# Merging transfers in a hybrid attention layer: spills, doubled loads, broadcast reciprocals, row statistics and mixed values

## The chip, the cores and the metric

The kernel runs on one core of a Trainium2 chip. The metric is the device time of one execution in microseconds (us). Before the change it was 1261.07 us, the median of 3 runs (1257.18 to 1261.21). A difference of about 0.3% is what a measurement of this kernel can tell from none.

## The reference

One decoder layer on 2048 tokens of width 1024, in float32:

```python
hdn  = rmsnorm(x, norm_gain)
proj = hdn @ w_in                 # q, k, v, gate of mixer A and of mixer B
q, k = rope(rmsnorm(q)), rope(rmsnorm(k))            # per head, both mixers
o_a  = banded_attention(q_a, k_a, v_a, 127, sinks)   # 8 heads, 2 kv heads
o_b  = dilated_attention(q_b, k_b, v_b)              # 8 heads
x    = x + concat([o_a * silu(g_a), o_b * silu(g_b)]) @ w_out
```

`banded_attention` lets a query read the keys of a causal band and returns its output, its row maximum and its softmax denominator. `dilated_attention` runs it three times, with (window, dilation) of (128, 1), (512, 4) and (2048, 16), on tokens gathered by stride, and merges the three outputs weighted by their denominators.

## The kernel before, in words

The layer is worked off in eight stages (`STAGES`, L26): four stages "B", each for two heads of mixer B, two stages "A", each for four heads of mixer A, and two stages "O" for the two halves of the output projection. A stage goes over four blocks `sb` of 512 tokens, a block over two halves of 256 tokens. Tokens are kept in a permuted order: within a block of 512, tokens of the same residue mod 4 lie together.

Every product of float32 values is made of three TensorE products (`mm3`, L241): both sides are split into a high and a low part. `proj` (L246) is a generator that makes the projections of a block step by step; while it runs, the attention units of earlier work are worked off between its steps (`advance`, L931), in a proportion set by hand-written costs. A unit has the steps scores, transposes, pv and after, and for a dilated unit a load that is called when the unit is among the next two pending. Actions on the list `late` are counted down in ticks and run some steps later. The compiler's planner then sets the order of the instructions on each engine by its own model of durations.

All transfers are issued by SyncE (`nc.sync.dma_start`) and so stand in one queue in the order of the program: a transfer that has to wait for a semaphore holds up those behind it. The steps that the change touches:

- **Spills** (`finish`, L342). At the end of a B block, q, k, the low parts of k, and the gate are stored to DRAM tensors `qd`, `kd`, `ld`, `gd`, so that the dilated units can read them back by residue r. For q and k there is one store for each of the two heads (L360, L362). V is stored as it is made (`vd`, L315): its source has 128 partitions, its destination is the access pattern [4, 32, 256] (residue, row, element).
- **Row statistics** (`units_B`, L750). The window units of a B block leave row maxima and denominators in `scB`. Four stores (L760), one for each residue, put them in `sd`, laid out [4, 32, 4, 4, 4], in runs of 16 bytes; one load of 32 KB (L859) reads them for the whole stage into `s1c` (128 partitions of 64 values).
- **Dilated loads** (`units_D`, L771, `load` in `dil`). A dilated unit for residue r and head h loads `cq`, `ck`, `cl` and `cv`, each with two buffers. The k of a head has 64 rows; it is needed twice, in partitions 0 to 63 and 64 to 127, and so `ck` (L785) and `cl` (L788) are each loaded by two transfers of 64 partitions x 2 KB. The scores' matmuls at L808 and L809 read them.
- **Broadcast reciprocals.** After its two dilated units, the weights of a residue are transposed to 16 rows, stored to a small DRAM tensor `rD` (L881), and read back with each row repeated over 64 partitions, in the tile `Rb` (one buffer): twice, for the two patterns (`bcast`, L887), each time by two transfers of 64 partitions. GpSimd multiplies with them at L899 and L904. In mixer A, `final` (L678) does the same with `rA`, once for each pair of heads, for the product at L688.
- **Mixed values.** The gated outputs are stored to `mx`, eight DRAM tensors (L93), one for each 256 tokens: four stores for a dilated residue (L909), two for a pair of heads of mixer A (L690). Stages "O" load them as their x (`x_load`, L145).

Of the kernel before, what the change touches and what calls it, by code (L numbers as in the profile page):

```python
# [18 lines left out]
KC = DM // 128  # L19
# [9 lines left out]
def f32(ap):  # L29
    return ap.bitcast(F32)  # L30
# [3 lines left out]
def hybrid_layer(ctx, tc, xT, xn, x, wB, wA, wO, ng, gains, sinks, rot, masks, ident, out):  # L34
# [55 lines left out]
                nc.gpsimd.tensor_scalar(zt, mk[z, 0:640], 0.0, None, op0=OP.mult)  # L90

    rs_row = [dram([256], f"rsr{hf}") for hf in range(8)]
    mx = [dram([128, KC, 256], f"mx{hf}") for hf in range(8)]  # L93

    def bcast_row(d, lo, n, parts=128):
        return bass.AP(tensor=d.tensor, offset=d.offset + lo, ap=[[0, parts], [1, n]])
# [131 lines left out]
    def spill_tiles(si):  # L228
        if si not in spill:
            spill[si] = {  # L230
                "q": dram([2, 4, 128, 512], f"qd{si}"),
                "k": dram([2, 4, 64, 512], f"kd{si}"),
                "l": dram([4, 128, 512], f"ld{si}"),
                "v": dram([4, 4, 128, 256], f"vd{si}"),
                "g": dram([4, 128, 512], f"gd{si}"),
                "o": dram([4, 128, 512], f"od{si}"),
                "s": dram([4, 32, 4, 4, 4], f"sd{si}"),
            }
        return spill[si]

# [101 lines left out]
    def finish(si, sb, half, hls):  # L342
        kind = STAGES[si][0]
        KK, KL = K[si, sb]
        nk = 1 if kind == "A" else 2
        if half == 0 and sb > 0:
            pk, pl = K[si, sb - 1]
            for h in range(nk):
                nc.scalar.activation(KK[:, h, :, 0, :], f32(pk[:, h, :, 4, :]), AF.Copy)
            for h in range(nk):  # L350
                hs = slice(64 * h, 64 * h + 64)
                nc.scalar.activation(KL[hs, h, :, 0, :], f32(pl[hs, h, :, 4, :]), AF.Copy)
        yield from qk_transposes(si, sb, half, hls)
        if half == 0:
            return
        if kind == "B":
            d = spill_tiles(si)
            cs = slice(sb * 128, sb * 128 + 128)
            for h in range(2):
                nc.sync.dma_start(d["q"][h][:, :, cs].rearrange("r p c -> p r c"),  # L360
                                  f32(Q[si, sb][1][:, h]))
                nc.sync.dma_start(d["k"][h][:, :, cs].rearrange("r p c -> p r c"),  # L362
                                  f32(KK[:64, h, :, 1:5, :]).rearrange("p r i u -> p r (i u)"))
            for h in range(2):
                hs = slice(64 * h, 64 * h + 64)
                nc.sync.dma_start(d["l"][:, hs, cs].rearrange("r p c -> p r c"),
                                  f32(KL[hs, h, :, 1:5, :]).rearrange("p r i u -> p r (i u)"))
            nc.sync.dma_start(d["g"][:, :, cs].rearrange("r p c -> p r c"),
                              G[si, sb][0].rearrange("p r i u -> p r (i u)"))
            pending.extend(units_B(si, sb))  # L370
            if sb == 3:
                pending.extend(units_D(si, 0))
        else:
            pending.extend(units_A(si, sb))
# [281 lines left out]
    def units_A(si, sb):  # L656
        idx = STAGES[si][1]
        sc = wk.tile([128, 2, 4, 4], F32, name="scA")
        units = []
        osum = {}  # L660

        def rows(p):
            e = wk.tile([128, 2, 4], F32, name="eA")
            hs = slice(2 * p, 2 * p + 2)
            nc.vector.tensor_tensor(e, sc[:, 0, hs], sk[:, 4 * idx + 2 * p:4 * idx + 2 * p + 2, None].to_broadcast([128, 2, 4]),
                                    op=OP.add)
            nc.scalar.activation(e, e, AF.Exp)
            nc.vector.tensor_tensor(e, e, sc[:, 1, hs], op=OP.add)
            nc.vector.reciprocal(e, e)
            pr = ps.tile([8, 128], F32, name="po", bufs=2)  # L670
            nc.tensor.transpose(pr, e.rearrange("p h i -> p (h i)"), idf)
            rr = wk.tile([16, 128], F32, name="rr")
            nc.scalar.activation(rr[:8], pr, AF.Copy)
            d = dram([8, 128], f"rA{si}_{sb}_{p}")
            nc.sync.dma_start(d, rr[:8])
            osum["d", p] = d

        def final(p):  # L678
            d = osum["d", p]
            rb = wk.tile([128, 512], F32, name="Rb", bufs=1)  # L680
            for a in range(2):
                nc.sync.dma_start(rb[64 * a:64 * a + 64, :],
                                  bass.AP(tensor=d.tensor, offset=d.offset + a * 512, ap=[[0, 64], [1, 512]]))
            t = osum[p]
            g = G[si, sb][p].rearrange("p r i u -> p (r i u)")
            nc.gpsimd.tensor_tensor(t, t, g, op=OP.mult)
            mix = wk.tile([128, 512], F32, name="o1c", bufs=1)
            nc.gpsimd.tensor_tensor(cm_view(mix), cm_view(t), to_cm(rb), op=OP.mult)  # L688
            for a in range(2):
                nc.sync.dma_start(mx[2 * sb + a][:, 2 * idx + p, :], mix[:, 256 * a:256 * a + 256])  # L690

        for p in range(2):
            units.extend(pair_units(si, sb, p, sc, osum, rows, final))
        return units
# [55 lines left out]
    def units_B(si, sb):  # L750
        sc = wk.tile([128, 4, 2, 2], F32, name="scB")
        osum = wk.tile([128, 512], F32, name="osum", bufs=3)
        d = spill_tiles(si)
        units = []
        for h in range(2):
            def after(h=h):
                if h == 1:
                    with nc.allow_non_contiguous_dma(reason="row statistics"):
                        for r in range(4):
                            nc.sync.dma_start(d["s"][:, :, sb, r, :].rearrange("i u k -> u i k"),  # L760
                                              sc[32 * r:32 * r + 32].rearrange("p i a h -> p i (a h)"))
                    cs = slice(sb * 128, sb * 128 + 128)
                    nc.sync.dma_start(d["o"][:, :, cs].rearrange("r p c -> p r c"), osum.rearrange("p (r c) -> p r c", r=4))
            stats = ([sc[:, i, 0, h:h + 1] for i in range(4)], [sc[:, i, 1, h:h + 1] for i in range(4)])
            units.append(window_unit(si, sb, h, stats, cm_view(osum[64 * h:64 * h + 64, :]), after))
        return units


    S1 = {}

    def units_D(si, r):  # L771
        d = spill_tiles(si)
# [3 lines left out]
        def dil(h):  # L776
# [3 lines left out]
            def load():  # L780
                q = wk.tile([128, 512], F32R, name="cq")
                nc.sync.dma_start(f32(q), d["q"][h, r])
                k = wk.tile([128, 512], F32R, name="ck")
                for a in range(2):
                    nc.sync.dma_start(f32(k[64 * a:64 * a + 64, :]), d["k"][h, r])  # L785
                kl = wk.tile([128, 512], F32R, name="cl")
                for a in range(2):
                    nc.sync.dma_start(f32(kl[64 * a:64 * a + 64, :]), d["l"][r, hp:hp + 64, :])  # L788
                v = wk.tile([128, 4, 128], F32R, name="cv")
                nc.sync.dma_start(f32(v), d["v"][r][:, :, 128 * h:128 * h + 128].rearrange("t p e -> p t e"))  # L790
                s["v"], s["q"], s["k"], s["kl"] = v, q, k, kl
# [62 lines left out]
            def after():  # L854
                if h == 0:
                    return
                if (si) not in S1:
                    t = wk.tile([128, 4, 4, 4], F32, name="s1c")
                    nc.sync.dma_start(t.rearrange("p s r k -> p (s r k)"), d["s"].rearrange("i u s r k -> (i u) (s r k)"))  # L859
                    S1[si] = t  # L860
                s1 = S1[si]
                A = s1[:, :, r, :].rearrange("p t (k h) -> p k h t", k=2)
# [23 lines left out]
                o2 = c["o2"]  # L886
                def bcast(k):  # L887
                    rb = wk.tile([128, 512], F32, name="Rb", bufs=1)
                    for a in range(2):
                        nc.sync.dma_start(rb[64 * a:64 * a + 64],  # L890
                                          bass.AP(tensor=dd.tensor, offset=dd.offset + 1024 * k + a * 512, ap=[[0, 64], [1, 512]]))
                    return rb

                def first():
# [8 lines left out]
                def third(rb):  # L903
                    nc.gpsimd.tensor_tensor(o2, o2, rb, op=OP.mult)  # L904
                    nc.gpsimd.tensor_tensor(o2, o2, o1, op=OP.add)
                    nc.gpsimd.tensor_tensor(o2, o2, gc, op=OP.mult)
                    ch = 4 + STAGES[si][1]
                    for t_ in range(4):
                        nc.sync.dma_start(mx[2 * t_ + r // 2][:, ch, 128 * (r % 2):128 * (r % 2) + 128],  # L909
                                          o2[:, 128 * t_:128 * t_ + 128])  # L910

                late.append([2, first])

# [126 lines left out]
```

## Time and profile before

| what | value |
|---|---|
| time, median of 3 runs | 1261.07 us (1257.18 to 1261.21) |
| time of the profiled execution | 1261.51 us |
| its span, first to last instruction | 1259.4 us |
| TensorE matmul busy | 1174.8 us, 93% of the span |
| VectorE, ScalarE, GpSimd busy | 850.7, 834.7, 680.4 us |
| granted TensorE clock | 0.969 |
| DMA queue q1 | 219.37 MB, its packets took 59.3% of the 16 DMA engines' time |
| chain that ended last | PE 55%, DMA 16%, DVE 10%, ACT 8%, POOL 6%, issue 3%, SPq 2% |

PE is TensorE, DVE VectorE, ACT ScalarE, POOL GpSimd, SP or SPq SyncE and its queue. L785 is line 785 of the kernel. In names such as `ck<-kd`, the tile written stands before the arrow and what is read behind it. The chain that ended last is followed back from the last instruction, at each step to what released it; a share of it is time in which that engine, or a transfer's landing, was what the end waited for. A share of DMA is the part of the time for which the 16 DMA engines worked on packets; a packet is one run of bytes that one engine moves.

### The profile page before, as it was taken

Reading aid. Unit: us, or ns where it says so; the run is one execution under the profiler, and the core shown is the slowest. Engines: PE = TensorE matmul, PEld = TensorE weight load, DVE = VectorE, ACT = ScalarE, POOL = GpSimd, SP = SyncE. Lnnn points to the kernel's source line nnn. Section 1 sums busy time; section 2 is a strip of 40 time slices with the busy share of each in tenths; the row PEclk is TensorE's granted clock in tenths of the full one; section 3 lists DMA queues with packets and bytes.
Section 4 is the critical chain, followed back from the end, with each engine's and each line's share of the span. In section 5 each row is a group of like instructions: output and inputs, shape, how many; then the busy total and the mean of one; then the engine's idle time right before and its main releaser. Section 6 shows DMA issues by size and latency. Waiting matters only on the chain.

```text
span 1259.4 us, 25438 instructions
## 1 busy us (share of the span) xinstructions
PE 1174.8 (93%) x8328; PEld 1141.3 (91%) x8328; DVE 850.7 (68%) x2288; ACT 834.7 (66%) x2418; POOL 680.4 (54%) x788
## 2 busy tenths in 40 slices
PE   6898979899899798899998999999999999999899
PEld 5898979899799798888997999898899998999898
DVE  5676768678677678776777788789868877522221
ACT  6477868678677687676777677677776776522221
POOL 4886734566645574536576567565655554333122
PEclk9899989999899899899998999999999999999999
DMA  7454677877687667687775764545333225566561
GB/s 215 120 166 127 193 226 212 229 200 212 182 250 207 210 190 201 189 244 204 199 210 172 228 203 143 150 137 167 114 97 94 80 89 165 163 192 211 166 191 69
DMA packets 196883, 220.98 MB, mean 175 GB/s; under 512 B 34312, under 2 KB 143632, under 8 KB 196752
## 3 DMA queue, kind: packets, MB, share of 16 engines
q1 hardware_dynamic: 196752, 219.37, 59.3%
q8 instruction: 66, 1.08, 0.4%
q14 instruction: 65, 0.53, 0.1%
HBM read 164.44 MB, written 54.86 MB: 174 GB/s over the span
## 4 chain that ended last, share of the span: by engine, by line
PE 55%; DMA 16%; DVE 10%; ACT 8%; POOL 6%; issue 3%; SPq 2%; POOLq 0%; ACTq 0%; DVEq 0%
PE pj L244 39%; DMA xs<-in_xT 3%; DMA Rb<-rD 2%; DMA stg<-in_wB 2%; PE po L849 2%; DMA stg<-in_wO 2%; DMA stg<-in_wA 2%; PE sc L590 1%; PE sc L591 1%; PE po L645 1%; PE pt L828 1%; PE po L735 1%; PE pt L719 1%; ACT P L599 1%; DVE ptl L574 1%
## 5 line engine op out<-in xcount | busy, mean ns | idle before, releaser
L244 PE MATMUL pj<-wh,xh 128*128 128x384 f32 (+1 forms) x1008 | 332.8, 332 | 12.2 <-ACT wh L104 5.5
L244 PE MATMUL pj<-wl,xh 128*128 128x384 f32 (+1 forms) x1008 | 334.4, 332 | 0.8 <-DVE wl L102 0.7
L244 PE MATMUL pj<-wh,xl 128*128 128x384 f32 (+1 forms) x1008 | 333.4, 331 | 1.3 <-DVE xl L157 1.3
L157 POOL TENSOR_TENSOR xl<-xs,xh 128x512 fp32r<-128x512 f32 x158 | 210.3, 1341 | 146.3 <-ACT xh L155 136.6
L155 ACT ACTIVATE xh<-xs 128x512 fp32r<-128x512 f32 x252 | 154.5, 629 | 123.6 <-PE pj L244 100.6
L244 PEld LDWEIGHTS pj<-wh,xh 128*128 128x128 f32 x1008 | 194.0, 193 | 15.7 <-ACT wh L104 5.8
L244 PEld LDWEIGHTS pj<-wl,xh 128*128 128x128 f32 x1008 | 194.8, 193 | 3.2 <-DVE wl L102 1.1
L244 PEld LDWEIGHTS pj<-wh,xl 128*128 128x128 f32 x1008 | 194.4, 193 | 3.0 <-DVE xl L157 1.6
L574 DVE TENSOR_TENSOR ptl<-pt,pth 128x512 fp32r<-128x512 f32 (+3 forms) x232 | 142.0, 619 | 35.5 <-ACT pth L573 31.8
L244 PE MATMUL pj<-xh,wgh 128*128 128x256 f32 x496 | 147.7, 298 | 17.9 <-DVE V L311 12.0
L244 PE MATMUL pj<-xh,wgl 128*128 128x256 f32 x496 | 145.8, 294 | 0.0
L244 PE MATMUL pj<-xl,wgh 128*128 128x256 f32 x496 | 145.4, 293 | 0.0
L573 ACT ACTIVATE pth<-pt 128x512 fp32r<-128x512 f32 (+3 forms) x232 | 123.1, 543 | 23.1 <-PE pt L719 8.1
L431 POOL TENSOR_TENSOR t<-t,t 128x256 f32<-128x256 f32 (+1 forms) x96 | 78.1, 814 | 77.9 <-DVE t L422 57.2
L244 PEld LDWEIGHTS pj<-xh,wgh 128*128 128x128 f32 x496 | 97.8, 197 | 19.7 <-ACT klz L502 5.9
L244 PEld LDWEIGHTS pj<-xl,wgh 128*128 128x128 f32 x496 | 97.8, 197 | 0.6
L244 PEld LDWEIGHTS pj<-xh,wgl 128*128 128x128 f32 x496 | 97.4, 196 | 0.9 <-DVE wgl L105 0.2
L814 ACT ACTIVATE P<-P,scD 128x256 f32<-128x256 f32 (+3 forms) x128 | 71.6, 560 | 33.6 <-DVE scD L813 32.9
L157 DVE TENSOR_TENSOR xl<-xs,xh 128x512 fp32r<-128x512 f32 x94 | 76.9, 823 | 21.1 <-ACT xh L155 20.5
L447 DVE TENSOR_TENSOR t<-t,fac 128x256 f32<-128x256 f32 (+1 forms) x96 | 67.4, 710 | 30.8 <-POOL fac L182 23.7
L182 POOL TENSOR_TENSOR fac<-un,mhalf 128x8 f32<-128x8 f32 (+1 forms) x48 | 85.4, 1779 | 2.5
L813 DVE CUSTOM_DVE_ANT_0 P<-sc,mk 128x256 f32<-128x256 f32 (+3 forms) x128 | 61.1, 484 | 32.2 <-PE sc L809 31.5
(188 smaller groups left out, 3082.8 us busy)
## 6 DMA issues: line engine op xcount, KB each, us to landing
xs<-in_xT SPq DMA_DIRECT2D x94, 512.0 KB
xs<-mx SPq DMA_DIRECT2D x32, 512.0 KB
vd<-V SPq DMA_DIRECT2D x64, 128.0 KB
qd<-qc SPq DMA_DIRECT2D x32, 256.0 KB
TT<-tab SPq DMA_DIRECT2D x32, 256.0 KB
cv<-vd SPq DMA_DIRECT2D x32, 256.0 KB
cq<-qd SPq DMA_DIRECT2D x32, 256.0 KB
ck<-kd SPq DMA_DIRECT2D x64, 128.0 KB
```

The costliest lines, as they stand in the source:

```text
L155: nc.scalar.activation(h, f, AF.Copy)
L157: eng.tensor_tensor(l, f, f32(h), op=OP.subtract)
L182: nc.gpsimd.tensor_tensor(y, u, mhalf.to_broadcast([128, n]), op=OP.pow)
L244: nc.tensor.matmul(o, a, b, start=first and n == 0, stop=last and n == 2, skip_group_check=True)
L431: nc.gpsimd.tensor_tensor(t1[:, :n], t1[:, :n], t2[:, :n], op=OP.add)
L447: nc.vector.tensor_tensor(t1v, t1v, fac[:, tt, :, None].to_broadcast([128, nh, 64]), op=OP.mult)
L573: nc.scalar.activation(hi, pt, AF.Copy)
L574: nc.vector.tensor_tensor(lo, pt, f32(hi), op=OP.subtract)
L590: nc.tensor.matmul(sc[:, j, :], q[h // 2][:, h % 2, i, :], kw, start=True, stop=False)
L813: nc.vector.tensor_tensor_reduce(pd, o[:, :m], m2[:, 512 - m:], -0.125, BIG, OP.add, OP.min, nb)
L814: nc.scalar.activation(pd, pd, AF.Exp, bias=nb, scale=-1.0, accum_out=l)
L849: nc.tensor.matmul(po[:, o:o + w], a, b, start=n_ == 0, stop=n_ == len(seq) - 1, skip_group_check=True)
```

## The change

Transfers that move several parts of one tensor are made one:

- the q and k spills of both heads: one store each, with head and residue as one dimension;
- the two halves of `ck`, and of `cl`: one load of 128 partitions from a source that is read twice by a leading dimension of 2 with step 0 (`twice`);
- the two halves of `Rb`: one load from a source [2, 64 with step 0, 512];
- the row statistics: one store of 128 partitions x 64 bytes for each block, in a layout [4, 128, 16]; the gathering is moved to the load, which becomes four loads of 32 partitions in runs of 16 bytes;
- the mixed values: `mx` becomes one DRAM tensor with a leading dimension of 8, and the four or two stores one.

The diff, with unchanged lines left out:

```diff
-    mx = [dram([128, KC, 256], f"mx{hf}") for hf in range(8)]
+    mx = dram([8, 128, KC, 256], "mx")
...
-                "s": dram([4, 32, 4, 4, 4], f"sd{si}"),
+                "s": dram([4, 128, 16], f"sd{si}"),
...
-            for h in range(2):
-                nc.sync.dma_start(d["q"][h][:, :, cs].rearrange("r p c -> p r c"),
-                                  f32(Q[si, sb][1][:, h]))
-                nc.sync.dma_start(d["k"][h][:, :, cs].rearrange("r p c -> p r c"),
-                                  f32(KK[:64, h, :, 1:5, :]).rearrange("p r i u -> p r (i u)"))
+            nc.sync.dma_start(d["q"][:, :, :, cs].rearrange("h r p c -> p (h r) c"),
+                              f32(Q[si, sb][1]).rearrange("p h r c -> p (h r) c"))
+            nc.sync.dma_start(d["k"][:, :, :, cs].rearrange("h r p c -> p (h r) c"),
+                              f32(KK[:64, :, :, 1:5, :]).rearrange("p h r i u -> p (h r) (i u)"))
...
-            for a in range(2):
-                nc.sync.dma_start(rb[64 * a:64 * a + 64, :],
-                                  bass.AP(tensor=d.tensor, offset=d.offset + a * 512, ap=[[0, 64], [1, 512]]))
+            nc.sync.dma_start(rb, bass.AP(tensor=d.tensor, offset=d.offset, ap=[[512, 2], [0, 64], [1, 512]]))
...
-            for a in range(2):
-                nc.sync.dma_start(mx[2 * sb + a][:, 2 * idx + p, :], mix[:, 256 * a:256 * a + 256])
+            nc.sync.dma_start(mx[2 * sb:2 * sb + 2, :, 2 * idx + p, :].rearrange("a p n -> p a n"),
+                              mix.rearrange("p (a n) -> p a n", a=2))
...
-                        for r in range(4):
-                            nc.sync.dma_start(d["s"][:, :, sb, r, :].rearrange("i u k -> u i k"),
-                                              sc[32 * r:32 * r + 32].rearrange("p i a h -> p i (a h)"))
+                        nc.sync.dma_start(d["s"][sb], sc.rearrange("p i a h -> p (i a h)"))
...
+    def twice(dst, src):
+        nc.sync.dma_start(dst, bass.AP(tensor=src.tensor, offset=src.offset, ap=[[0, 2]] + [list(x) for x in src.ap]))
...
-                for a in range(2):
-                    nc.sync.dma_start(f32(k[64 * a:64 * a + 64, :]), d["k"][h, r])
+                twice(f32(k), d["k"][h, r])
...
-                for a in range(2):
-                    nc.sync.dma_start(f32(kl[64 * a:64 * a + 64, :]), d["l"][r, hp:hp + 64, :])
+                twice(f32(kl), d["l"][r, hp:hp + 64, :])
...
-                    nc.sync.dma_start(t.rearrange("p s r k -> p (s r k)"), d["s"].rearrange("i u s r k -> (i u) (s r k)"))
+                    ds = d["s"]
+                    with nc.allow_non_contiguous_dma(reason="row statistics"):
+                        for i in range(4):
+                            nc.sync.dma_start(t[32 * i:32 * i + 32].rearrange("u s r k -> u (s r) k"),
+                                              bass.AP(tensor=ds.tensor, offset=ds.offset + 4 * i,
+                                                      ap=[[16, 32], [512, 16], [1, 4]]))
...
-                    for a in range(2):
-                        nc.sync.dma_start(rb[64 * a:64 * a + 64],
-                                          bass.AP(tensor=dd.tensor, offset=dd.offset + 1024 * k + a * 512, ap=[[0, 64], [1, 512]]))
+                    nc.sync.dma_start(rb, bass.AP(tensor=dd.tensor, offset=dd.offset + 1024 * k, ap=[[512, 2], [0, 64], [1, 512]]))
...
-                    for t_ in range(4):
-                        nc.sync.dma_start(mx[2 * t_ + r // 2][:, ch, 128 * (r % 2):128 * (r % 2) + 128],
-                                          o2[:, 128 * t_:128 * t_ + 128])
+                    nc.sync.dma_start(mx[r // 2::2, :, ch, 128 * (r % 2):128 * (r % 2) + 128].rearrange("t p n -> p t n"),
+                                      o2.rearrange("p (t n) -> p t n", t=4))
```

## The prediction

> **What bounds the kernel now.** I read the page's totals first, then the table of stretches, then the chain of waits, then the DMA views.
>
> ```profile
> span 1259.4 us, 25438 instructions
> PE 1174.8 (93%) x8328; PEld 1141.3 (91%) x8328; DVE 850.7 (68%) x2288; ACT 834.7 (66%) x2418; POOL 680.4 (54%) x788
> DMA packets 196883, 220.98 MB, mean 175 GB/s; under 512 B 34312, under 2 KB 143632, under 8 KB 196752
> q1 hardware_dynamic: 196752, 219.37, 59.3%
> PE 55%; DMA 16%; DVE 10%; ACT 8%; POOL 6%; issue 3%; SPq 2%; POOLq 0%; ACTq 0%; DVEq 0%
> ```
>
> TensorE is busy for 93% of the span and holds 55% of the chain that ended last; SyncE's own issuing (SPq) holds 2% of it, about 25 us. All transfers go through one hardware queue, q1, whose packets keep the 16 DMA engines busy for 59.3% on average. So PE sets the time, with DMA landings (16% of the chain) as its main interruptions. The profiled execution took 1261.51 us (2.1 us around the span), 0.04% from the median of 1261.07, so sums made against it need no correction.
>
> The table of stretches (start:end, length, busy time of PE, PEld, DVE, ACT, POOL, clock, DMA share, GB/s) shows where DMA has least room:
>
> ```profile
> 172.00:880.00 708.00, 661.74 (x4540) 640.42 (x4539) 532.86 (x1482) 525.32 (x1548) 409.67 (x482) 0.96 0.69 198
> 880.00:1010.00 130.00, 127.16 (x925) 123.06 (x925) 100.70 (x297) 94.42 (x304) 73.46 (x80) 1.00 0.31 98
> ```
>
> From 172 to 880 us the dilated units run (their loads, the broadcast reciprocals); there the engines are 69% busy as a mean, and PE 661.74 of 708 us. There is 31% of slack if transfers stay spread over all 16 engines, and none if many land on a few.
>
> **How a transfer is spread.** This is the point on which the forecast turns, and the trace can be made to tell it. The list of DMA issues has 48 rows that add up to 1136 transfers; these are its first, those with a special shape, and its last:
>
> ```profile
> xs<-in_xT SPq DMA_DIRECT2D x94, 512.0 KB
> ...
> vd<-V SPq DMA_DIRECT2D x64, 128.0 KB
> ...
> TT<-in_rot SPq DMA_DIRECT2D x16, 128.0 KB
> ...
> sd<-scB SPq DMA_DIRECT2D x64, 2.0 KB
> ...
> rA<-rr SPq DMA_DIRECT2D x16, 4.0 KB
> ...
> rsr<-RB SPq DMA_DIRECT2D x8, 1.0 KB
> s1c<-sd SPq DMA_DIRECT2D x4, 32.0 KB
> ...
> ngt<-in_ng SPq DMA_DIRECT2D x1, 4.0 KB
> sk<-in_sinks SPq DMA_DIRECT2D x1, 4.0 KB
> ```
>
> By their shapes, the data runs under 512 B are sd 64 x 128, s1c 4 x 128, TT<-in_rot 16 x 512, and ngt and sk 128 each: 17,152. The page counts 34,312 packets under 512 B, so 17,160 small packets are not data. One completion packet per engine and transfer would make 1136 x 16 = 18,176; 1016 are missing. That is exactly 64 x 12 + 16 x 8 + 8 x 15: the vd stores, whose destination counts 4 in its outermost dimension, run on 4 engines, the rA stores (8 rows) on 8, the rsr stores (1 row) on 1, all others on 16. An access pattern's outermost count limits the engines, although the other side of vd has 128 partitions.
>
> **The change part by part.**
>
> *Doubled dilated loads (`twice`, ck and cl).* Two issues of 128 KB become one of 256 KB whose source is led by a dimension of 2 with step 0. The 128 issues become 64 merged loads. *Broadcast reciprocals (Rb):* the source is now led by [512, 2]; 64 issues from rD become 32, and 32 from rA become 16. By the count just made, each of these 112 merged transfers runs on 2 engines, and each of the two moves 64 rows of 2 KB, 131,072 bytes, where 16 engines moved 8 rows each before. The rate of one engine comes from q1's packets, bytes and share in three windows: 172 to 880, 1200 to 1250 (few small packets, some queueing) and 1180 to 1185 us (almost none):
>
> ```profile
> q1 hardware_dynamic: 137961, 139.41, 68.7%
> q1 hardware_dynamic: 2929, 6.96, 42.0%
> q1 hardware_dynamic: 368, 0.66, 35.5%
> ```
>
> 139.41 MB / (0.687 x 16 x 708 us) = 17.9 KB/us; 6.96 / (0.42 x 16 x 50) = 20.7; 0.66 / (0.355 x 16 x 5) = 23.2. A merged transfer holds its two engines for 7.3, 6.3 or 5.6 us, against about 0.8 us on each of 16 at 20.7.
>
> Now the stretch 172 to 880. It contains all ck, cl and rD transfers and, of rA, these:
>
> ```profile
> ck<-kd SPq DMA_DIRECT2D x64, 128.0 KB
> cl<-ld SPq DMA_DIRECT2D x64, 128.0 KB
> Rb<-rD SPq DMA_DIRECT2D x64, 128.0 KB
> vd<-V SPq DMA_DIRECT2D x47, 128.0 KB
> Rb<-rA SPq DMA_DIRECT2D x8, 128.0 KB
> ```
>
> So 32 + 32 + 32 + 4 = 100 merged transfers, 26.2 MB, that is 13.1 MB on each of two engines. The rest, 139.4 - 26.2 = 113.2 MB, puts 7.08 MB on every engine; the 47 vd stores put 1.16 MB more than an even share on four engines. If the two are always the same, and among vd's four, they carry 13.1 + 7.08 + 1.16 = 21.3 MB: 920 us of work at 23.2, 1031 at 20.7, 1192 at 17.9, in a stretch of 708. It grows by 212, 323 or 484 us. No row names the engine of a packet; I take the same two, since nothing in the rows suggests a rotation, and leave the other to a rival. I take the middle rate: the high one would need no queueing and two engines that never idle, the low one today's contention on all 16, which falls when 14 of them wait. **+323 us.** PE, with 662 us of work there, then waits for the two engines.
>
> [...]
>
> What is late next shows in the chain of waits around 404 us (start, length, what) and in the waits of that stretch:
>
> ```profile
> 404.46 5.18 DMA vd<-V
> ...
> 410.59 3.47 DMA rD<-rr
> ...
> 414.62 3.58 DMA Rb<-rD
> ...
> 418.34 1.30 POOL o1c L899
> ...
> 420.18 4.38 DMA Rb<-rD
> POOL o1c L899 <- DMA Rb<-rD: 58.3, 15, 8.2
> DVE P L813 <- PE sc L809: 31.5, 28, 3.4
> SPq L890 <- DMA rD<-rr: 34.7, 14, 5.3
> ```
>
> SyncE waits for rD to land before it issues Rb, and for POOL's L899 before the second Rb; behind it in its queue stand the next xs, cq and ck loads. Each Rb landing grows by some 5.5 us (6.3 - 0.8) plus the backlog, and every 16-engine transfer behind it lands only when its shares on the two loaded engines do. Those waits are how the stretch is stretched; they are inside the +323, not on top of it.
>
> *After 880* twelve merged rA broadcasts remain at +5.5 us, 66 us if each were on the path, nothing if POOL's idle time hid all. The engines are 31% busy there, and PE 127 of 130 us; a landing that is late by 5.5 us is mostly hidden by POOL's 44% of idle time, so a quarter: **+16 us**. Without that cover it is the 66.
>
> *Spills of q and k, mixed values, row statistics.* q and k spills: 64 issues become 32; mixed values: 64 become 16 and 32 become 16; both are rewritten with the partition outermost on both sides (128, or 64 for k), so 16 engines and the same runs. Row statistics: 64 stores become 16 with runs of 64 B in place of 16 B; 4 loads become 16 of 512 runs of 16 B: 10,240 small runs against 8704, all on 16 engines. In all 244 fewer of the 1136 issues:
>
> ```profile
> L785 SPq DMA_DIRECT2D ck<-kd x64: 444/473/1381, 172.6 to 787.2; - x64
> L890 SPq DMA_DIRECT2D Rb<-rD x64: 444/509/678, 211.7 to 869.8; - x64
> L760 SPq DMA_DIRECT2D sd<-scB x64: 302/426/1807, 86.7 to 703.8; - x64
> ```
>
> At about 0.47 us an issue (medians, ns) that is 115 us of SyncE's time, but SyncE mostly waits for others; of the chain it is 25 us, and 244/1136 of that is **-5 us** (bounds 0 and -25). `mx` as one tensor could make a mixed-value store wait, at the head of SyncE's queue, for an earlier one where its eight parts were tracked apart: such a wait is 2.5 us by the nearest row (34.7 us in 14 for L890), so 80 us for the 32 stores, and 0 if regions are told apart. I take 0, since an earlier store has long landed when the next is made, and keep the 80 as a bound.
>
> Sum: 1261.5 + 323 + 16 - 5 = 1595 us. Its own range: 1261.5 + 212 - 25 = 1450 to 1261.5 + 484 + 66 + 80 = 1890, the last only with all upper ends at once.
>
> **The rivals.**
>
> 1. *Not slower: the write side alone sets the spread.* In all three shapes that the trace shows on few engines, the destination is the short side, or both are; no row has a short source before a 128-partition destination, as here. If the source does not count, all merged transfers stay on 16 engines, 244 issues go, and each Rb pair lands one issue (0.51 us) sooner on some of the 32 rD steps: -5 to -25, about 1246 us. It decides if the number of completion packets stays at 16 for ck, cl and Rb. Against it: a source led by 2 has to be cut somehow, and vd shows that the shorter of the two counts won. 10%.
>
> 2. *Latency only: two engines per transfer, but different ones.* Then no pair of engines overflows, and each merged landing is just 5.5 us later. The whole chain has Rb<-rD 2.5% (31.5 us, some nine landings of 3.58): +50; the 28 waits of L813 behind the scores that read ck and cl: +154 if all grow. Between them about +100: 1360 us. For it: no row names the engines. Against it: a rotation would have to be kept somewhere. 10%.
>
> 3. *Worse: the two engines also idle.* SyncE, in order, stands at L890 while they drain. If they were busy for only 80% of the stretch, 1031 / 0.8 = 1289 us, +581: 1850 us. For it: the SP waits above, and PE and DMA each waiting for the other with two buffers per name. Against it: a backlog of 10 us outlasts most of those waits (5.3 us at the longest). 8%.
>
> ```profile
> by line: PE pj L244 38.9%; issue 3.5%; DMA xs<-in_xT 2.6%; DMA Rb<-rD 2.5%; DMA stg<-in_wB 2.2%; PE po L849 2.1%; DMA stg<-in_wO 1.9%; DMA stg<-in_wA 1.6%; PE sc L590 1.4%; PE sc L591 1.4%; PE po L645 1.3%; PE pt L828 1.3%; PE po L735 1.3%;
> ```
>
> **How the numbers follow.** Forecast 72%, rivals 10, 10 and 8%. The range reaches from 1400 (the forecast's low end, and the upper part of rival 2) to 1800: it leaves out rival 1, most of rivals 2 and 3, and of the forecast only its far upper end. About 0.3% is what a measurement of this kernel can tell from no change. Faster takes most of rival 1 (7%), the same its rest and a rival 2 that is hidden (4%), slower the remaining 89%.
>
> **What would show it.** Right: 892 issues with 892 x 16 - 1016 - 112 x 14 = 11,688 completions and 18,688 small data runs, 30,376 packets under 512 B; the mean DMA share falls while the span grows; Rb, ck and cl landings of 7 us and more head the chain of waits; the growth lies between the first dilated load and the last, and the stretches before 172 us hardly change. Rival 1: 31,944 such packets, and unchanged landings. Rival 2: two completions, but PE's idle time only next to L808, L899 and L904. The forecast is wrong in size if the stretch of the dilated units grows by less than 212 or more than 484 us.

## The result, and the profile after

The changed kernel takes 1625.22 us (median of 4 runs, 1624.22 to 1628.3), against 1261.14 us before (median of 4). The ratio is 1.2888, with a 95% interval of 1.2837 to 1.2938: slower by 364 us. The forecast was 1595 us in a range of 1400 to 1800.

The page of the kernel after, the lines that answer to the first fence of the prediction:

```profile
span 1623.0 us, 25100 instructions
PE 1248.7 (77%) x8328; PEld 1205.8 (74%) x8328; DVE 829.6 (51%) x2288; ACT 837.8 (52%) x2418; POOL 666.9 (41%) x788
DMA packets 192945, 220.94 MB, mean 136 GB/s; under 512 B 30376, under 2 KB 139696, under 8 KB 192816
q1 hardware_dynamic: 192816, 219.35, 45.1%
DMA 34%; PE 30%; issue 9%; POOL 8%; ACT 8%; DVE 7%; SPq 4%; POOLq 0%; ACTq 0%; DVEq 0%
```

Packets under 512 B are 30,376, the number that the prediction gave for two engines per merged transfer (31,944 would have meant 16). The same bytes are moved, the mean busy share of the DMA engines falls from 59.3 to 45.1%, and yet DMA landings are now 34% of the chain that ended last and PE only 30%: the DMA engines as a whole are emptier, and the end waits for a few of them.

The tables of stretches follow, with the columns of the prediction's table (start:end, length, PE, PEld, DVE, ACT, POOL, clock, DMA share, GB/s). The first is of after: first dilated load to last mixed-value store of a dilated residue, then the rest, then what lies before. The second is of before, for the two parts that the prediction did not show:

```profile
168.00:1222.00 1054.00, 725.68 (x4553) 694.43 (x4551) 512.20 (x1483) 528.06 (x1550) 395.24 (x481) 0.83 0.45 133
1222.00:1623.00 401.00, 375.78 (x2840) 366.90 (x2840) 203.03 (x535) 191.03 (x548) 155.27 (x148) 0.96 0.41 129
0.00:168.00 168.00, 147.28 (x937) 144.51 (x938) 114.37 (x272) 118.76 (x321) 116.42 (x159) 0.92 0.59 171
```

```profile
0.00:172.00 172.00, 146.81 (x953) 142.84 (x954) 115.90 (x277) 119.92 (x327) 115.65 (x159) 0.94 0.58 170
880.00:1259.00 379.00, 366.22 (x2839) 358.07 (x2838) 201.95 (x530) 189.47 (x544) 155.06 (x148) 0.99 0.43 136
```

The stretch of the dilated units grew from 708 to 1054 us (+346), the rest from 379 to 401 (+22), and what lies before changed by -4. Counting the packets of q1 in the traces tells what filled the added time: exactly two packets are in flight for 351 of these 1054 us, against 11 of the 708 before. By the small packets a merged transfer has two engines, so nearly all of the added time, 340 of 346 us, is time in which only two DMA engines work.

The chain that ended last in after, where the first dilated loads are made (start, length, what):

```profile
174.91 14.94 DMA cq<-qd
...
201.86 13.12 DMA cl<-ld
...
226.26 9.78 DMA xs<-in_xT
...
239.55 9.78 DMA rD<-rr
```

Some of its longer waits (who waited for what: us in total, times, longest):

```profile
POOL o1c L898 <- DMA Rb<-rD: 217.0, 15, 24.3
...
DVE P L809 <- PE sc L805: 123.8, 33, 19.3
...
SPq L890 <- DMA rD<-rr: 64.7, 16, 8.1
SPq L890 <- DMA Rb<-rD: 59.4, 12, 7.2
```

The shapes of cq, xs and rD were not touched, and by the count of 30,376 small packets they still run on 16 engines. They land after 9.8 to 14.9 us; before, the chain had 3.5 us for rD. That some of their shares stand behind merged transfers is the reading that fits; the view of one line below supports it. SyncE shows a second thing. Its timeline (start, length of the issue, line, count) at the same place:

```profile
168.39 1.19 SPq L767 DMA_DIRECT2D ck<-kd  x1
169.67 0.78 SPq L767 DMA_DIRECT2D cl<-ld  x1
170.50 4.35 SPq L767 DMA_DIRECT2D ck<-kd  x1
174.91 5.44 SPq L780 DMA_DIRECT2D cq<-qd  x2
180.39 1.34 SPq L767 DMA_DIRECT2D cl<-ld  x1
181.78 5.36 SPq L148 DMA_DIRECT2D xs<-in_xT  x1
...
202.52 10.58 SPq L858 DMA_DIRECT2D s1c<-sd  x4
```

An issue takes about 0.45 us in the median, before and after; here single issue instructions last 4.4 and 5.4 us. All issues added took 544 us for 1136 transfers before and 704 us for 892 after.

By 174.9 us, then, three merged transfers have been issued (`ck`, `cl`, `ck`). In the window 173 to 180 us q1 shows this (packets, MB, share of the 16 DMA engines):

```profile
q1 hardware_dynamic: 173, 0.35, 12.8%
```

12.8% of 16 is 2.05 engines. Merged transfers on different pairs would have kept four or six engines busy, 25% or more. So these merged transfers, queued together, ran on the same two engines, one after the other, and the other fourteen had nothing to do in this window. The two moved 0.35 MB in 7 us, 25 KB/us each: at that rate, a merged transfer alone holds them for 5.2 us, an estimate from the 131,072 bytes that each of them moves for it.

### The profile page after: what moved, and what is told of

Its sections match the earlier page's. It is cut to its first block, busy times and chain, and to the rows that moved or that the text cites. A ratio compares the mean times of both kernels' runs of the same rounds, so it can differ in the third digit from the quotient of the medians.

```text
span 1623.0 us, 25100 instructions
## 1 busy us (share of the span) xinstructions
PE 1248.7 (77%) x8328; PEld 1205.8 (74%) x8328; DVE 829.6 (51%) x2288; ACT 837.8 (52%) x2418; POOL 666.9 (41%) x788
## 2 busy tenths in 40 slices
DMA packets 192945, 220.94 MB, mean 136 GB/s; under 512 B 30376, under 2 KB 139696, under 8 KB 192816
## 3 DMA queue, kind: packets, MB, share of 16 engines
q1 hardware_dynamic: 192816, 219.35, 45.1%
## 4 chain that ended last, share of the span: by engine, by line
DMA 34%; PE 30%; issue 9%; POOL 8%; ACT 8%; DVE 7%; SPq 4%; POOLq 0%; ACTq 0%; DVEq 0%
PE pj L244 22%; DMA Rb<-rD 7%; DMA xs<-in_xT 4%; DMA rD<-rr 4%; DMA cl<-ld 4%; DMA Rb<-rA 3%; DMA cq<-qd 3%; DMA stg<-in_wB 2%; DMA stg<-in_wO 2%; ACT P L598 2%; POOL fac L182 2%; SPq L767 1%; DMA cv<-vd 1%; DVE ptl L573 1%; ACT xh L155 1%
## 5 line engine op out<-in xcount | busy, mean ns | idle before, releaser
L244 PE MATMUL pj<-wh,xh 128*128 128x384 f32 (+1 forms) x1008 | 343.8, 343 | 43.1 <-DVE G L332 24.2
L244 PE MATMUL pj<-wh,xl 128*128 128x384 f32 (+1 forms) x1008 | 342.1, 340 | 8.6 <-POOL xl L157 8.3
L244 PE MATMUL pj<-wl,xh 128*128 128x384 f32 (+1 forms) x1008 | 341.6, 339 | 0.8 <-DVE wl L102 0.7
L244 PEld LDWEIGHTS pj<-wh,xh 128*128 128x128 f32 x1008 | 201.6, 201 | 48.0 <-DVE G L332 24.8
L244 PEld LDWEIGHTS pj<-wh,xl 128*128 128x128 f32 x1008 | 201.9, 200 | 10.6 <-POOL xl L157 9.1
L809 DVE CUSTOM_DVE_ANT_0 P<-sc,mk 128x128 f32<-128x128 f32 (+3 forms) x128 | 61.0, 484 | 140.3 <-PE sc L805 123.8
L810 ACT ACTIVATE P<-P,scD 128x128 f32<-128x128 f32 (+3 forms) x128 | 71.5, 559 | 110.0 <-DVE scD L809 109.7
L244 PEld LDWEIGHTS pj<-xh,wgh 128*128 128x128 f32 x496 | 104.8, 211 | 22.9 <-ACT ob L734 9.5
L898 POOL TENSOR_TENSOR o1c<-o1c,Rb 128x512 f32<-128x512 f32 x16 | 20.4, 1272 | 223.6 <-DMA Rb<-rD 217.0
L804 PE MATMUL sc<-ck,cq 128*128 128x256 f32 (+2 forms) x128 | 48.2, 382 | 76.2 <-DMA cq<-qd 45.6
```

Of the source, the lines that this page charges most:

```text
L244: nc.tensor.matmul(o, a, b, start=first and n == 0, stop=last and n == 2, skip_group_check=True)
L804: nc.tensor.matmul(o, q[:, qs], k[:, :n], start=True, stop=False)
L809: nc.vector.tensor_tensor_reduce(pd, o[:, :m], m2[:, 512 - m:], -0.125, BIG, OP.add, OP.min, nb)
L810: nc.scalar.activation(pd, pd, AF.Exp, bias=nb, scale=-1.0, accum_out=l)
```

## The experiments

The differences below are between medians, each against runs of the kernel before that were made together with it. The compiler's planner orders the instructions anew for each version, so a difference can also come from the order. In the traces, TensorE's order differs from that of before at 42% of its places in the first run below and at 52% in the run with k on 128 rows, and these two are within 0.4% of before: a new order alone need not cost anything.

**The rest of the change alone.** The kernel after, with the merged loads undone:

```diff
-                twice(f32(k), d["k"][h, r])
+                for a in range(2):
+                    nc.sync.dma_start(f32(k[64 * a:64 * a + 64, :]), d["k"][h, r])
...
-                twice(f32(kl), d["l"][r, hp:hp + 64, :])
+                for a in range(2):
+                    nc.sync.dma_start(f32(kl[64 * a:64 * a + 64, :]), d["l"][r, hp:hp + 64, :])
...
-            nc.sync.dma_start(rb, bass.AP(tensor=d.tensor, offset=d.offset, ap=[[512, 2], [0, 64], [1, 512]]))
+            for a in range(2):
+                nc.sync.dma_start(rb[64 * a:64 * a + 64, :],
+                                  bass.AP(tensor=d.tensor, offset=d.offset + a * 512, ap=[[0, 64], [1, 512]]))
...
-                    nc.sync.dma_start(rb, bass.AP(tensor=dd.tensor, offset=dd.offset + 1024 * k, ap=[[512, 2], [0, 64], [1, 512]]))
+                    for a in range(2):
+                        nc.sync.dma_start(rb[64 * a:64 * a + 64],
+                                          bass.AP(tensor=dd.tensor, offset=dd.offset + 1024 * k + a * 512, ap=[[0, 64], [1, 512]]))
```

> The kernel after with ck, cl and Rb taken back to two 64-partition transfers each; the merged spills, row statistics and mixed values stay. Theory (two engines carry the merged ck, cl and Rb): the whole loss goes, and 132 fewer issues than before leave 1261 - 5, between 1240 and 1262 us. Rival (the rest of the change, a wait on mx or the 16-byte gather, has a part in it): stays above 1280.

Measured: 1258.38 us, 1.0036 times before (1.0005 to 1.0067). The whole loss goes with the merged loads; spills, statistics and `mx` cost nothing that matters. The small gain that was expected of 132 fewer issues is not there either: if anything, the sign is the other one.

**The doubled loads alone**, in the kernel before:

```diff
-                for a in range(2):
-                    nc.sync.dma_start(f32(k[64 * a:64 * a + 64, :]), d["k"][h, r])
+                twice(f32(k), d["k"][h, r])
...
-                for a in range(2):
-                    nc.sync.dma_start(f32(kl[64 * a:64 * a + 64, :]), d["l"][r, hp:hp + 64, :])
+                twice(f32(kl), d["l"][r, hp:hp + 64, :])
```

> The kernel before with only ck and cl merged (64 transfers on two engines). Theory, by occupancy of two engines between 172 and 880 us: 122.6 MB / 16 + 1.16 + 64 x 0.131 = 17.2 MB on each of the two, 831 us at 20.7 KB/us against 708: +123, about 1385 us. Rival, a fixed delay for each merged transfer (364 us / 112 = 3.25 us): +208, about 1470.

Measured: 1487.39 us, 1.1868 times before (1.1816 to 1.1919), +233 us. That is more than the occupancy of the stretch gave (+123), and nearer to a fixed delay per transfer (3.6 us each). The tile view of this run tells what GpSimd waited for before it used Rb, whose own loads were left as they were:

```profile
  DMA Rb<-rD: 176.5, 26
```

Before the change it was 75.1 us in 22 waits:

```profile
  DMA Rb<-rD: 75.1, 22
```

Rb's own loads run on 16 engines here (the page has 32,392 packets under 512 B, that is 34,312 - 128 x 16 + 64 x 2), so they are most likely late because of others on two. This speaks against the second rival, in which a merged transfer only delays who reads it.

**The broadcasts alone**, in the kernel before, first those from rD, then those from rA:

```diff
-                    for a in range(2):
-                        nc.sync.dma_start(rb[64 * a:64 * a + 64],
-                                          bass.AP(tensor=dd.tensor, offset=dd.offset + 1024 * k + a * 512, ap=[[0, 64], [1, 512]]))
+                    nc.sync.dma_start(rb, bass.AP(tensor=dd.tensor, offset=dd.offset + 1024 * k, ap=[[512, 2], [0, 64], [1, 512]]))
```

> The kernel before with only the Rb loads from rD merged (32 transfers on two engines). Theory, occupancy: 131 MB / 16 + 1.16 + 32 x 0.131 = 13.5 MB, 654 us at 20.7 KB/us, which still fits in 708: no overflow, only the later landings, 0 to +50: 1261 to 1310 us. Rival, a fixed delay of 3.25 us each: +104, about 1365.

> The kernel before with only the Rb loads from rA merged (16 transfers on two engines, most after the dilated units). Theory, the term of the sum: +16 us, with bounds 0 and +88 (5.5 us for each of 16). Rival, a fixed delay of 3.25 us each: +52, about 1313.

Measured: 1379.72 us for rD (1.1022, 1.0972 to 1.1072; +125 us, 3.9 us for each of 32) and 1286.48 us for rA (1.0268, 1.0233 to 1.0302; +32 us, 2.0 for each of 16). The rD run fits into the stretch by mean occupancy and should have lost 50 us at the most; it lost more than the fixed delay gave. The three parts add up to 390 us where the whole change lost 364: the loss was close to additive in these runs, and showed no threshold at full occupancy. In the rA run TensorE, VectorE and ScalarE execute their instructions in exactly the order of before, so its 32 us owe nothing to the planner. In the rD run, the issues on SyncE were not held (536 us for 1104). Its waits and GpSimd's timeline show another way in which time goes:

```profile
POOL o1c L897 <- DMA Rb<-rD: 129.7, 15, 13.8
...
DVE t L447 <- POOL fac L182: 91.7, 15, 12.2
...
POOL osum L902 <- DMA Rb<-rD: 52.4, 9, 8.0
```

```profile
422.85 1.29 POOL L897 TENSOR_TENSOR o1c<-o1c,Rb 128x512 f32<-128x512 f32 x1 [12.60 <-DMA Rb<-rD]
424.08 0.41 POOL L479 CAST qc<-Q 128x256 fp32r<-128x256 f32 x1
424.44 0.74 POOL L431 TENSOR_TENSOR t<-t,t 128x256 f32<-128x256 f32 x1
433.17 1.28 POOL L902 TENSOR_TENSOR osum<-osum,Rb 128x512 f32<-128x512 f32 x1 [7.99 <-DMA Rb<-rD]
```

GpSimd, in order, stands 12.6 and 8.0 us before the two products; the rotary sums (L431), the q copies (L479) and later the norm factors (`fac`) stand behind. VectorE's wait for `fac` was 23.7 us before:

```profile
DVE t L447 <- POOL fac L182: 23.7, 9, 5.7
```

**Later use of Rb.** To test that, the rD run with the uses put off:

```diff
-                    late.append([3, lambda: second(rb)])
+                    late.append([6, lambda: second(rb)])
...
-                    late.append([3, lambda: third(rb)])
+                    late.append([6, lambda: third(rb)])
```

> As the run with only rD's Rb merged (+125 us), but second and third, which use Rb on GpSimd, are put on the late list with 6 ticks in place of 3. Theory (GpSimd, in order, stands at L899 and L904 until the two engines have delivered, and fac and xl wait behind it): the use comes after the landing, and the loss falls below +60 us. Rival (the two engines' occupancy costs the time): it stays near +125.

Measured: 1372.7 us, 1.09 times before (1.0872 to 1.0928), +113 us. The loss stayed, but the test did not take hold. GpSimd's waits for Rb are as long as without the edit:

```profile
POOL o1c L897 <- DMA Rb<-rD: 116.4, 14, 14.3
...
DVE t L447 <- POOL fac L182: 99.6, 16, 13.2
POOL osum L902 <- DMA Rb<-rD: 79.9, 13, 8.7
```

From issue to use is 8.5 us in the median, against 8.4 in the rD run: issue and use were moved together. So it stays open how much of the 125 us is GpSimd's order and how much is other transfers behind Rb.

**The hold by itself.** In the kernel before, two transfers were added behind each dilated load. They copy k from DRAM into rows of DRAM that nothing reads, so that no engine waits for their data:

```diff
+                for n in range(2):
+                    spare = dram([2, 64, 520], f"spare{si}_{r}_{h}_{n}")
+                    nc.sync.dma_start(spare[:, :, :512], bass.AP(tensor=d["k"].tensor, offset=d["k"][h, r].offset, ap=[[0, 2], [512, 64], [1, 512]]))
```

> The kernel before, all its own transfers as they were, plus two transfers of 256 KB behind each of the 32 dilated loads: DRAM to DRAM, rows of 2 KB, source led by 2 with step 0, destination two blocks of 64 rows that nothing reads. Theory, occupancy of the same two engines: 139.4 MB / 16 + 1.16 + 64 x 0.131 = 18.3 MB on each of the two, 882 us at 20.7 KB/us against 708: +174, about 1435 us, although nobody waits for these transfers. Rival, latency only: what nobody waits for costs nothing but its 64 issues, 1261 to 1275 us.

In the second run, `for a in range(2): nc.sync.dma_start(spare[a, :, :512], d["k"][h, r])` stands in place of the transfer:

> The same extra bytes, but as four transfers of 64 rows for each dilated load, each spread over 16 engines. Theory: 156.2 MB / 16 = 9.8 MB on each engine, 545 us at 17.9 KB/us, fits in 708: 1261 to 1290 us, the rise being that of contention and of 128 more issues. Rival (the bytes themselves or the writes to DRAM cost the time, not where they run): as slow as with two engines.

In the next three, 2 and 64 in the shapes are replaced by 4 and 32, by 8 and 16, and by 2 and 32 (half the bytes):

> As the run with extra transfers on two engines (which cost +298 us), but each source is led by 4 with step 0 over 32 rows: the same 64 x 256 KB, 32 rows of 2 KB on each of four engines. Theory A (each transfer delays what is queued behind it by its hold on its engines, linear between the +27 us of 16 engines and the +298 of two): hold halved, about +143 us. Theory B (SyncE's issue is held only when an engine's queue is full, so a threshold): less than half of +143. Theory C (mean occupancy over the stretch, as in the prediction): 14.1 MB on each of four, 680 us in 708: 0 to +27.

> The same, led by 8 over 16 rows: 16 rows on each of eight engines. Theory A: about +65 us. Theories B and C: as with all engines, +20 to +35.

> Two engines again, but half the bytes: led by 2 over 32 rows, 128 KB a transfer, 32 rows on each of the two. If the hold on the engines is what costs, and not how many are left over or the bytes in all, this is as the run on four engines within 40 us; if a narrow transfer is slow as such, it stays near +298.

| extra transfers (64 in all) | rows of 2 KB on each engine | time, ratio (interval) | loss | for each |
|---|---|---|---|---|
| 16 engines (two halves each) | 8 | 1282.15, 1.0207 (1.0178 to 1.0235) | 27 us | 0.42 us |
| 8 engines | 16 | 1309.82, 1.0404 (1.0375 to 1.0433) | 50 us | 0.78 us |
| 4 engines | 32 | 1388.57, 1.1008 (1.0967 to 1.1048) | 128 us | 2.0 us |
| 2 engines, half the bytes | 32 | 1372.5, 1.0903 (1.0861 to 1.0944) | 112 us | 1.8 us |
| 2 engines | 64 | 1553.38, 1.2363 (1.2335 to 1.239) | 298 us | 4.7 us |

The pages of the two-engine and the four-engine run confirm the spread, with 34,312 + 64 x 2 and 34,312 + 64 x 4 small packets:

```profile
DMA packets 205204, 237.78 MB, mean 153 GB/s; under 512 B 34440, under 2 KB 143760, under 8 KB 205072
```

```profile
DMA packets 205332, 237.78 MB, mean 171 GB/s; under 512 B 34568, under 2 KB 143888, under 8 KB 205200
```

The first and the last line of the table move the same bytes. What no engine reads costs 298 us on two engines and 27 on sixteen, so neither the bytes nor a reader's wait is the cause. The runs with two, four and eight engines have the same order of instructions on every engine, so between these three only the shape differs; the other two runs are ordered otherwise. Four engines, and two with half the bytes, agree within 16 us: what counted in these runs is how many rows stand in a row on one engine. The loss was somewhat more than proportional to it. Set against a hold of 82 ns a row (2 KB at the 25 KB/us above) it is 0.6 of the hold for 16 rows and 0.9 for 64. Mean occupancy allowed at most 27 us for four engines and 35 for eight, a threshold at a full queue less than 72 for four; measured were 128 and 50, so both fall. A delay in proportion to the hold was expected to cost 143 and 65, which is nearest.

One thing does wait for these transfers: SyncE. In the run with two engines its own waits have rows such as this, 59.5 us in 22 waits in all; with eight engines they are 32.8 us, with sixteen there are none:

```profile
SPq L788 <- DMA spare<-kd: 12.4, 4, 5.0
```

The semaphore numbers in the traces tell why. All transfers of these kernels count on eight semaphores in turn: every reuse comes eight transfers later (all 1128 reuses in the kernel before, all 884 in the kernel after), and most issues (1023 of 1192 reuses in this run) stand behind a recorded wait for the landing of the transfer that used the semaphore before. So transfers that nothing reads stopped the queue here, in the row above for up to 5.0 us. What more semaphores would change was not tested.

**k on 128 rows.** As the first run, but the spill of k is taken from all 128 partitions of the tile, which holds k twice, and ck is one plain load:

```diff
-                "k": dram([2, 4, 64, 512], f"kd{si}"),
+                "k": dram([2, 4, 128, 512], f"kd{si}"),
...
-                              f32(KK[:64, :, :, 1:5, :]).rearrange("p h r i u -> p (h r) (i u)"))
+                              f32(KK[:, :, :, 1:5, :]).rearrange("p h r i u -> p (h r) (i u)"))
...
-                for a in range(2):
-                    nc.sync.dma_start(f32(k[64 * a:64 * a + 64, :]), d["k"][h, r])
+                nc.sync.dma_start(f32(k), d["k"][h, r])
```

> As the run with the rest merged, but k is spilled on 128 rows (the tile holds it twice), so that ck is one plain load of 128 partitions on 16 engines: 32 fewer issues, 4.2 MB more stored. Theory (one issue for the doubled load is harmless when its outermost count is 128): within 0.5% of the run with the rest merged. Rival (one 256 KB load in place of two of 128 KB is itself late): clearly slower.

Measured: 1253.67 us, 0.9986 times before (0.9963 to 1.0008): no difference. The page has 33,224 packets under 512 B, 32 x 16 fewer than the 33,736 of the first run, so ck runs on 16 engines. One load in place of two, with an outermost count of 128, cost nothing here; and it gained nothing.

**The v spill on 16 engines.** If rows in a row on one engine cost, then so do the v stores of the kernel before, which run on four. On top of the last run:

```diff
-                vt = st.tile([128, nk, 2, 64], F32R, name="V", bufs=10)
+                if i == 0:
+                    vb = st.tile([128, 4, nk, 2, 64], F32R, name="V", bufs=3)
+                vt = vb[:, i]
...
-                if kind == "B":
+                if kind == "B" and i == 3:
                     d = spill_tiles(si)
-                    nc.sync.dma_start(d["v"][:, sb, i * 32:i * 32 + 32, :],
-                                      f32(vt).rearrange("p h a d -> p (h a d)"))
+                    for r in range(4):
+                        nc.sync.dma_start(d["v"][r, sb].rearrange("(i u) e -> u i e", u=32),
+                                          f32(vb[32 * r:32 * r + 32]).rearrange("p i h a d -> p i (h a d)"))
```

> As the run with k on 128 rows, and the v spill, which ran on four engines since its destination is led by 4, is made after a block's last projection as four stores by residue, each led by 32 on both sides, so on 16 engines; V is one tile for a block, and rr, s1c, eD and tD have one buffer to make room. If a hold on few engines costs in the kernel before too (64 stores of 32 rows of 1 KB on each of four, 1.6 us in place of 0.4): up to 50 us faster than before, 1205 to 1250. Rival (these holds are short enough to be hidden, and the stores now come late and together): within 1% of before.

Measured: 1242.87 us, 0.992 times before (0.9898 to 0.9943): 11 us faster, the only version here that beats both kernels. Its packets under 512 B, 33,992, are 64 x 12 more than in the run with k on 128 rows (33,224), so the v stores do run on 16 engines. Their number is the same, 64. They also come later, the buffers and the planner's order differ, and 0.8% lies within both expectations, so the spread is a possible cause and not a shown one.

## Why the prediction was right, point by point

- **The spread** is shown: 30,376 small packets as predicted, 11,688 of them of 4 bytes in the trace (17,160 before), and the counts of all runs above agree with their shapes. One transfer of 128 partitions in place of two of 64 cost nothing for k on 128 rows (0.9986 times before), and much where the source is led by 2 (1.1868 for `ck` and `cl`, 1.1022 for `Rb` from rD).
- **The +323 for the dilated stretch**: measured +346. The size was right, the step under it failed: "they carry 13.1 + 7.08 + 1.16 = 21.3 MB ... in a stretch of 708", a balance of two engines over the whole stretch. The rD run had room in that balance and lost 125 us; the doubled loads were due +123 and lost 233; extra transfers on four and eight engines were due at most 27 and 35 and lost 128 and 50. What the runs showed in its place is a loss of 2.0 to 3.9 us on average for each merged transfer, with parts that add up (233 + 125 + 32 = 390 us against 364). That fits a local delay, in which each holds up what is queued behind it on its engines. The slack of 31% was an average; little of another time's idleness could be used. The reading that fits is that a transfer on 16 engines needs a share of the held ones (cq, xs and rD landed after 9.8 to 14.9 us), and that SyncE, whose issues stand in one queue, waits for landings eight transfers back (675 of 884 reuses stand behind such a wait in the kernel after). That the size came out is in part luck: at the 25 KB/us that the two engines reached alone, the same balance is 852 us of work, +144. The prediction's slower rate made up for time that its balance did not have, in which the two were not both busy: at most one packet is in flight for 98 of the 1054 us.
- **The rates of 17.9 to 23.2 KB/us**: alone, an engine moved 25 KB/us (window 173 to 180), more than the highest of the three; its rate beside other transfers was not measured by itself. **The same two engines**: shown for the transfers queued behind each other in that window, by its 12.8%; which two, no row names.
- **+16 us after 880**: the rest of the kernel grew by 22, and the rA run by 32 for all sixteen; inside the bounds, and under-sized.
- **-5 us for fewer issues**: not found, 1.0036 in the run with 132 fewer. SyncE's time for normal issues seems not to be what the end waits for. `mx` as one tensor cost nothing that shows, as taken.
- **The rivals.** Not slower: refuted by the packet count. Latency only, on different engines: refuted by the added transfers, which nothing reads, and by the share of two engines in the window. Idle beyond the two engines' work: the time ended 225 us short of its 1850, but some such idle time there was (the 98 us above).
- **What was not in the sum**: TensorE's busy time rose by 74 us at the same number of matmuls, 64 of these us in the dilated stretch, where the granted clock is 0.83 after and 0.96 before, and TensorE is busy for 69% of the time in place of 93%. Why the clock was lower, no run here shows. With PE waiting for DMA this need not have lengthened the end; that was not tested.

## What to carry to other kernels

Before merging transfers, look at the outermost count of both access patterns: the smaller one limited the engines in every shape here (1, 2, 4, 8), and the number of small packets on the page told how many were used. Transfers with many rows on one engine cost time here even when no engine read them and the DMA engines were half idle on average (298 us for 64 transfers of 64 rows on each of two engines, at a mean share of 49.8%). The reading that fits is that a wide transfer behind them waits for the slowest of its shares (9.8 to 14.9 us for cq, xs and rD in the kernel after), and that SyncE, which waits for landings eight transfers back (59.5 us in 22 waits for the added transfers), cannot run far ahead. Judge such a transfer by its hold against the local lead of the next loads, not by mean occupancy; and where a kernel has such a narrow transfer already, spreading it is worth a try (11 us with the v stores, of which the spread is a possible cause).

## What the runs showed of the hardware that was not expected

SyncE's issue instruction itself was held while merged transfers were outstanding (4.4 and 5.4 us in the timeline of the kernel after, against a median of about 0.45). The added transfers' issues (min/median/max in ns) in the kernel with two engines and with eight:

```profile
L793 SPq DMA_DIRECT2D spare<-kd x64: 582/654/6208, 176.1 to 1007.9; - x64
```

```profile
L793 SPq DMA_DIRECT2D spare<-kd x64: 618/671/2498, 175.0 to 775.4; - x64
```

All issues added take 810 us for 1200 transfers with two engines, 647 with four, 591 with eight, and 627 for 1264 with sixteen. So with the backlog on two engines SyncE was also kept from feeding the others, beyond its waits for semaphores. Which limit is reached, the rows do not tell; with eight engines an issue takes 0.49 us in the mean, as with sixteen (0.50). In the rD run, where merged transfers come one at a time, their issues were not held (549 ns in the median, 569 at most), and the loss for each was as high (3.9 us): the held issue is one way of the delay and not the only one.
